# Query latents beside the first norm in a hybrid attention layer: the opening dealt anew

## The chip, the cores and the metric

The kernel runs on one core of one Trainium2 chip. The metric is the device time of one execution in microseconds; the time of a kernel is the median of its runs. Three runs of the kernel before took 2032.35, 2032.49 and 2034.26 us.

## What is computed

One layer of a streaming encoder on 1024 frames of width 1024, all in float32:

```
h  = rms_norm(x, ln_mix_pre)
z  = h @ w_in            # [q | k | v of 8 differential heads | q latent 384 | kv latent 256 | k rope 64 | 2 x 1024 gate logits]
branch A: 8 heads, o1 - lam * o2 of two softmax maps, rotary q and k, rms_norm per head
branch B: 8 heads from the latents: rms_norm(cq) @ w_uq, rms_norm(ckv) @ w_ukv, rotary part
x  = x + rms_norm((sigmoid(g_a) * (A @ w_proj_a) + sigmoid(g_b) * (B @ w_proj_b)) @ w_o)
x  = x + rms_norm((silu(h2 @ w_gate) * (h2 @ w_up)) @ w_down),   h2 = rms_norm(x)
```

Attention is causal by chunks of 64 frames. The change touches only the order in which the parts of z are made.

## The kernel before, in words

**Arithmetic.** Every float32 operand of a matmul is held as two fp32r parts: a high part, cast by ScalarE, and a low part, the rest, made by VectorE or POOL (`split_sbuf`, L252 to L256; `split_psum`, L258 to L261). One product is three matmuls, high by high, high by low, low by high (`mm3`, L266 to L269). So in the trace L267, L268 and L269 are the matmuls of nearly all projections, told apart by their columns: 384 for a differential head's projection and for the query latents, 320 for the kv latents, 512 for gate tiles.

**Memory.** Two large SBUF buffers, AR (split operands) and AFm (float32), are divided into zones. A zone hands out the piece that has been free for the longest time. Weights of projections come through `f_raw` (room for eight pieces of 384 columns) into `z_w` (8192 columns of AR); one set of eight 384-column weights takes 6144 of them. x tiles, tables, latents and other float32 pieces come from `f_gen`, 8448 columns. PSUM has eight banks: in the opening banks 0 to 5 serve the first head's projection, banks 6 and 7 all transposes. In the heads 0 to 3 hold scores, 4 and 5 projections.

**Order.** The parts are generators, written out by hand in the order wanted; the framework then fixes the order of every engine when the program is built, from the program's order, taking forward what it holds to be ready. Engines run their own lists in order, and all DMAs are issued from the one queue of SP, in order too.

**The opening.** `norm_x` goes through the eight x tiles of 128 rows, from 7 down to 0: load, sum of squares (ScalarE, L439), 1/rms (VectorE L245, POOL L247), multiply (VectorE, L441), eight transposes on TensorE (L447), split of two banks into hT (L260, L261). `rotary_tables` makes cosines and sines on VectorE in ten steps (L331 to L366). `da_proj(0)` projects the first differential head: eight weight pieces of 128 x 384, loaded at L546 as three strips of 128 columns and split with every second low half on POOL; then for each tile 24 matmuls, rotary steps on VectorE (`rope`, L385 to L390), splits, and transposes of K (L592). Before the change one step of the tables stands on either side of each tile of the norm, and then the projection is drained. `lambda_column` makes a scalar for the differential heads.

**The heads.** For each of the eight differential heads `interleave` runs the attention (first its small transposes at L689) together with fillers: gate tiles (48 matmuls of 512 columns each, with two weight pieces of 1024 columns), the query or the kv latents, and the projection of the next head. `FILL` names the fillers of each head, and a pace is summed from them: 10.4 for a gate tile, 33.6 and 28.0 for the latents, 32.4 for a projection. The pace only says how densely fillers stand between the attention's steps.

**The query latents.** `latents("cq")` loads eight weight pieces of 128 x 384 (L285), the latent norm's weights, and per tile does 24 matmuls, the sum of squares (L500), a multiply out of PSUM (L502), and, one tile later, three transposes (L518), a copy, and a store to the scratch s_cq in DRAM. The latents are read again only after the last differential head. All its low halves of weights are made by VectorE.

What follows the differential heads (the latent attention, the two branch projections, the output projection and the channel part) is not touched.

Of the kernel before, what the change touches and what calls it, by code (L numbers as in the profile page):

```python
# [21 lines left out]
NT = S // P  # L22
# [37 lines left out]

W_ENG = "dve"
L_ENG = lambda nc: nc.vector
FILL = ((0, 1, 2, 3), (4, 5), ("cq",), ("ckv",), (6, 7), (8, 9), (10, 11, 12), (13, 14, 15))
PRE = 1
DA_DEPTH = 1
MLA_DEPTH = 2
# [103 lines left out]
def kernel(  # L170
# [122 lines left out]
    mr, mf, mp = Mem(AR, AR_COLS), Mem(AFm, AF_COLS), Psum(PS)  # L293
# [18 lines left out]
    ps_s, ps_p, ps_a = Banks(mp, 0, 4), Banks(mp, 4, 6), Banks(mp, 6, 8)  # L312
# [166 lines left out]
        for o in own:  # L479
            o.free()  # L480

    def latents(which):
        if which == "cq":
            lo, n, nw, nrm, dst = 3072, 384, 384, q_a_norm, s_cq
        else:
# [3 lines left out]
        nc.sync.dma_start(wb.ap, nrm[0].partition_broadcast(P))  # L489
        nb = nw // P  # L490
        late = None
        for t in reversed(range(NT)):
            sl = slice(t * P, (t + 1) * P)
            pb = ps_p.alloc()
            o = pb.ap[:, 0:n]
            for k in range(NK):
                mm3(o, hT[:, k, 0, sl], hT[:, k, 1, sl], w[k][0], w[k][1], k == 0, k == NK - 1)
# [268 lines left out]
    def drain(g):  # L766
        for c in g:
            assert c != "blocked"
# [556 lines left out]
    all_slots = [[None] * 4 for _ in range(NH + 1)]  # L1325
    nx, tab = norm_x(), rotary_tables()
    next(nx)
    next(tab)
    next(nx)
    first = da_proj(0, all_slots[0], Banks(mp, 0, 6))  # L1330
    next(first)
    for _ in range(NT):
        next(tab, None)
        next(nx, None)
        next(tab, None)
    drain(tab)
    drain(nx)
    neg_lam, sub8 = lambda_column()
    drain(first)
    M = Mla()  # L1340
    hs = [{} for _ in range(NH + 1)]

# [4 lines left out]
    for n in range(NH):  # L1347
        fl, pace = [], 0.0
        for f in FILL[n]:
            if f == "cq":  # L1350
                fl.append(latents("cq"))
                pace += 33.6
            elif f == "ckv":
                fl.append(latents("ckv"))
                pace += 28.0
            else:
                fl.append(gate_tile(f))
                pace += 10.4
        if n == NH - 1:
            fl += [after_ht(), mla_setup(M), mla_proj(M, 0, hs[0])]  # L1360
            pace += 35.0
        if n + 1 < NH:
            fl.append(da_proj(n + 1, all_slots[n + 1]))
            pace += 32.4
        interleave(da_attn(n, all_slots[n], neg_lam, sub8), fl, pace)
# [72 lines left out]
```

## Time and profile before

| what | value |
|---|---|
| median of three runs | 2032.49 us |
| time of the profiled execution | 2036.9 us |
| its span, first to last instruction | 2035.0 us |
| mean granted TensorE clock | 0.992 |

Busy shares of the page, in order: TensorE's matmuls, its weight loads, VectorE, ScalarE, POOL. On TensorE a row of a matmul lasts until its result is out, so that rows of matmuls in a series overlap; the distance of two starts tells the pace. On the page and in the windows, PE is TensorE's matmuls, PEld its weight loads, DVE VectorE, ACT ScalarE, and POOL GpSimd. A number behind x is a count. Behind a windows row's stretch stand its length, then busy time and count of each engine, the granted clock as a share of 2.4 GHz (1.00 also where the trace has no record of it), the busy share of the DMA engines and GB/s.

### The profile page before, as it was taken

What the parts mean: (1) busy time and instruction counts of PE and PEld (TensorE: products, weight loads), DVE (VectorE), ACT (ScalarE), POOL (GpSimd) and SP (SyncE); (2) the same over time, 40 slices, a digit from 0 to 9 for tenths busy, and PEclk for the clock granted to TensorE, in tenths of its full rate; (3) what the DMA queues carried; (4) which work ended last, traced back from release to release, by engine and by line L of the source; (5) the groups of instructions that cost most, each with busy time, mean ns of one, the idle gap of its engine ahead of it and who ended that gap; (6) DMA issues with size and microseconds to landing.
All of it is one profiled execution on the core that took longest, in us unless ns stands there. A gap on an engine that the chain in (4) does not pass through costs nothing. (4 is left out here: it accounts for less than half of the span.)

```text
span 2035.0 us, 29108 instructions
## 1 busy us (share of the span) xinstructions
PE 1976.3 (97%) x10656; PEld 1715.3 (84%) x10656; DVE 1156.2 (57%) x2464; ACT 864.2 (42%) x1912; POOL 541.0 (27%) x652
## 2 busy tenths in 40 slices
PE   6999999999999999999999998979999999999998
PEld 6898999999898988988978786757888888888886
DVE  7756757676675667786752354575344444353335
ACT  5445444554544446666653333343333333341102
POOL 2000010200000012222121222356564564462214
PEclk9999999999999999999999999989999999999999
DMA  5212111211212031450043533223222222272204
GB/s 169 69 47 81 44 55 53 57 49 42 77 29 80 29 116 50 130 177 29 32 136 103 176 125 103 85 71 94 73 94 84 71 95 73 95 237 83 83 32 145
DMA packets 148494, 176.52 MB, mean 87 GB/s; under 512 B 13536, under 2 KB 117376, under 8 KB 148352
## 3 DMA queue, kind: packets, MB, share of 16 engines
q1 hardware_dynamic: 148352, 174.68, 27.3%
q8 instruction: 83, 1.36, 0.3%
q14 instruction: 59, 0.48, 0.1%
HBM read 130.54 MB, written 44.11 MB: 86 GB/s over the span
## 5 line engine op out<-in xcount | busy, mean ns | idle before, releaser
L267 PE MATMUL PS<-AR 128*128 128x512 f32 (+3 forms) x2216 | 795.1, 361 | 4.0 <-ACT AR L254 2.5
L269 PE MATMUL PS<-AR 128*128 128x512 f32 (+3 forms) x2216 | 786.3, 356 | 2.6 <-POOL AR L256 2.6
L268 PE MATMUL PS<-AR 128*128 128x512 f32 (+3 forms) x2216 | 784.5, 355 | 3.7 <-POOL AR L256 3.7
L254 ACT CAST AR<-AFm 128x512 fp32r<-128x512 f32 (+4 forms) x514 | 301.7, 610 | 514.1 <-PE PS L1216 207.4
L267 PEld LDWEIGHTS PS<-AR 128*128 128x128 f32 x2216 | 418.1, 189 | 56.8 <-ACT AR L260 3.5
L268 PEld LDWEIGHTS PS<-AR 128*128 128x128 f32 x2216 | 419.0, 189 | 47.8 <-POOL AR L256 4.5
L269 PEld LDWEIGHTS PS<-AR 128*128 128x128 f32 x2216 | 417.9, 189 | 46.3 <-POOL AR L256 3.5
L256 POOL TENSOR_TENSOR AR<-AFm,AR 128x512 fp32r<-128x512 f32 (+4 forms) x203 | 309.2, 1529 | 461.7 <-ACT AR L254 397.4
L1216 PE MATMUL PS<-AR 128*128 128x512 f32 x1848 | 425.7, 392 | 6.1 <-POOL AR L256 4.9
L1216 PEld LDWEIGHTS PS<-AR 128*128 128x128 f32 x1848 | 349.3, 189 | 82.2 <-POOL AR L256 6.2
L256 DVE TENSOR_TENSOR AR<-AFm,AR 128x512 fp32r<-128x512 f32 (+5 forms) x311 | 213.1, 714 | 109.3 <-ACT AR L254 81.8
L260 ACT CAST AR<-PS 128x512 fp32r<-128x512 f32 (+3 forms) x320 | 134.5, 440 | 149.5 <-DVE AFm L388 75.4
L1225 DVE TENSOR_TENSOR AFm<-AFm,PS 128x512 f32<-128x512 f32 x110 | 75.2, 684 | 180.3 <-PE PS L1216 179.6
L261 DVE TENSOR_TENSOR AR<-PS,AR 128x512 fp32r<-128x512 f32 (+3 forms) x320 | 152.9, 496 | 38.0 <-ACT AR L260 36.5
L619 POOL CAST AR<-AR 128x128 fp32r<-128x128 f32 (+1 forms) x128 | 43.1, 337 | 456.0 <-PE PS L690 262.4
L649 ACT ACTIVATE AFm<-PS,nm 128x1024 f32<-128x1024 f32 (+3 forms) x192 | 142.5, 745 | 45.9 <-DVE nm L648 28.8
L648 DVE TENSOR_REDUCE nm<-PS 128x1 f32<-128x1024 f32 (+3 forms) x192 | 143.5, 751 | 3.2
L1288 DVE TENSOR_TENSOR AFm<-AFm,PS 128x512 f32<-128x512 f32 x80 | 54.4, 685 | 103.1 <-PE PS L269 103.1
L1180 DVE TENSOR_TENSOR AFm<-AFm 128x512 f32<-128x512 f32 x66 | 70.4, 1066 | 68.4 <-DMA s_aa<-AFm 29.7
L627 POOL MEMSET AR<- 128x256 f32 x64 | 22.3, 349 | 295.3 <-PE PS L269 200.3
L707 PE MATMUL PS<-AR 128*128 128x256 f32 x640 | 94.9, 290 | 0.1
L609 PE MATMUL PS<-idf,AFm 128*128 128x128 f32 x576 | 88.6, 275 | 2.2 <-ACT AFm L741 0.9
(133 smaller groups left out, 1551.9 us busy)
## 6 DMA issues: line engine op xcount, KB each, us to landing
AFm<-in_w_in_dram SPq DMA_DIRECT2D x72, 192.0 KB
AFm<-in_w_ffn_gate_dram SPq DMA_DIRECT2D x22, 512.0 KB
AFm<-in_w_ffn_up_dram SPq DMA_DIRECT2D x22, 512.0 KB
s_aa<-AFm SPq DMA_DIRECT2D x44, 256.0 KB
AFm<-in_w_ffn_down_dram SPq DMA_DIRECT2D x22, 512.0 KB
AFm<-s_aa SPq DMA_DIRECT2D x22, 512.0 KB
AFm<-in_x_dram SPq DMA_DIRECT2D x16, 512.0 KB
AFm<-in_w_in_dram SPq DMA_DIRECT2D x32, 256.0 KB
```

Source lines behind the costliest of these rows:

```text
L254: nc.scalar.copy(h, src)
L256: e.tensor_tensor(out=l, in0=src, in1=f32v(h), op=ALU.subtract)
L260: nc.scalar.copy(h, src)
L261: nc.vector.tensor_tensor(out=l, in0=src, in1=f32v(h), op=ALU.subtract)
L267: nc.tensor.matmul(o, lhsT=sh, rhs=mh, start=first, stop=False)
L268: nc.tensor.matmul(o, lhsT=sh, rhs=ml, start=False, stop=False)
L269: nc.tensor.matmul(o, lhsT=sl, rhs=mh, start=False, stop=last)
L609: nc.tensor.transpose(tb.ap[:, q * P:(q + 1) * P], C[:, (g + q) * P:(g + q + 1) * P], idf)
L648: nc.vector.tensor_reduce(out=nm[:, m:m + 1], in_=src, axis=ax, op=ALU.max, negate=True)
L649: nc.scalar.activation(out=dst, in_=src, func=ACTF.Exp, bias=nm[:, m:m + 1], scale=1.0, accum_out=ss[:, m:m + 1])
L707: nc.tensor.matmul(sb.ap[:, p * 256:(p + 1) * 256], lhsT=qs.ap[:, m * 256 + v * P:m * 256 + v * P + P], rhs=slots[p]["kT"][:, m, :], start ...
L1216: nc.tensor.matmul(o, lhsT=v[:, ws, k], rhs=m, start=first and k == 0 and x == 0, stop=k == 3 and x == 2, skip_group_check=True)
```

## The change

The query latents leave the fillers of the third head and go into the opening. They are loaded ahead of the norm's first tile, take six PSUM banks, and one tile of latents stands behind each tile of the norm. The tables start behind the second tile and take two steps behind each tile from the third on. The first differential head's projection, its weights' loads included, comes after all that. The gate tiles are dealt anew.

```diff
-FILL = ((0, 1, 2, 3), (4, 5), ("cq",), ("ckv",), (6, 7), (8, 9), (10, 11, 12), (13, 14, 15))
+FILL = ((0, 1, 2), (3, 4), (5, 6), ("ckv",), (7, 8), (9, 10), (11, 12), (13, 14, 15))
...
-    def latents(which):
+    def latents(which, banks=None):
+        banks = banks or ps_p
...
         nc.sync.dma_start(wb.ap, nrm[0].partition_broadcast(P))
         nb = nw // P
         late = None
+        if which == "cq":
+            yield 0.0
         for t in reversed(range(NT)):
             sl = slice(t * P, (t + 1) * P)
-            pb = ps_p.alloc()
+            pb = banks.alloc()
...
     nx, tab = norm_x(), rotary_tables()
     next(nx)
-    next(tab)
+    first = latents("cq", Banks(mp, 0, 6))
+    next(first)
     next(nx)
-    first = da_proj(0, all_slots[0], Banks(mp, 0, 6))
-    next(first)
-    for _ in range(NT):
-        next(tab, None)
+    for t in range(NT):
         next(nx, None)
-        next(tab, None)
+        next(first, None)
+        if t == 1:
+            next(tab)
+        elif t > 1:
+            next(tab, None)
+            next(tab, None)
+    drain(nx)
     drain(tab)
-    drain(nx)
+    drain(first)
     neg_lam, sub8 = lambda_column()
-    drain(first)
+    drain(da_proj(0, all_slots[0], Banks(mp, 0, 6)))
```

## Rows read from the trace of the kernel before

**Rows 1.** The page, part 1: busy us, share of the span, instructions

```profile
PE 1976.3 (97%) x10656; PEld 1715.3 (84%) x10656; DVE 1156.2 (57%) x2464; ACT 864.2 (42%) x1912; POOL 541.0 (27%) x652
```

**Rows 2.** Windows of the opening: stretch, PE, PEld, DVE, ACT, POOL, clock, DMA

```profile
0.00:11.75 11.75, 0.00 (x0) 0.00 (x1) 5.00 (x17) 4.54 (x8) 1.61 (x10) 1.00 0.81 227
11.75:16.81 5.06, 2.80 (x10) 2.07 (x10) 4.61 (x7) 3.60 (x8) 4.97 (x4) 1.00 1.08 333
16.81:21.09 4.28, 4.28 (x16) 4.18 (x17) 3.66 (x6) 2.22 (x5) 1.16 (x2) 1.00 0.34 114
21.09:61.57 40.48, 38.83 (x239) 37.12 (x239) 36.08 (x102) 22.65 (x50) 6.50 (x14) 1.00 0.32 93
```

**Rows 3.** Timeline of TensorE, 0 to 21 us: start, us, engine, line, operation

```profile
11.75 1.97 PE L447 MATMUL PS<-idf,AFm 128*128 128x128 f32 x8 [11.75 <-DVE rs_v L245]
...
16.81 1.12 PE L447 MATMUL PS<-idf,AFm 128*128 128x128 f32 x4 [2.26 <-DVE AR L261]
...
20.50 0.52 PE L269 MATMUL PS<-AR 128*128 128x384 f32 x1
...
20.82 0.47 PE L267 MATMUL PS<-AR 128*128 128x384 f32 x1
```

**Rows 4.** Windows cut at the starts of heads 0, 1, 2, 4, 5, 6

```profile
61.57:170.31 108.74, 108.67 (x643) 97.59 (x642) 68.48 (x191) 48.48 (x129) 5.52 (x18) 1.00 0.22 66
170.31:252.80 82.49, 82.49 (x527) 76.53 (x527) 56.77 (x158) 41.20 (x110) 5.93 (x21) 1.00 0.19 58
252.80:351.40 98.60, 97.28 (x647) 93.83 (x647) 63.80 (x177) 48.85 (x136) 9.74 (x29) 1.00 0.19 52
...
446.10:529.10 83.00, 83.00 (x524) 76.17 (x523) 56.24 (x156) 41.58 (x109) 6.20 (x21) 1.00 0.18 53
529.10:611.30 82.20, 82.20 (x520) 75.64 (x519) 55.93 (x155) 40.74 (x107) 5.77 (x20) 1.00 0.18 53
611.30:705.20 93.90, 93.65 (x569) 84.76 (x569) 56.79 (x156) 42.55 (x110) 5.75 (x21) 1.00 0.19 56
```

**Rows 5.** Timeline of TensorE, 24 to 62 us, for the pitch

```profile
24.10 1.04 PE L447 MATMUL PS<-idf,AFm 128*128 128x128 f32 x8
...
24.89 0.42 PE L267 MATMUL PS<-AR 128*128 128x384 f32 x1
...
60.35 0.34 PE L269 MATMUL PS<-AR 128*128 128x384 f32 x1
...
61.57 0.39 PE L267 MATMUL PS<-AR 128*128 128x512 f32 x1
```

**Rows 6.** First loads: the timeline of SP and ScalarE, and one window

```profile
2.27 0.43 SPq L432 DMA_DIRECT2D AFm<-in_ln_mix_pre_dram  x1
4.51 1.06 ACT L439 ACTIVATE AFm<-AFm 128x1024 f32<-128x1024 f32 x1 [2.50 <-DMA AFm<-in_x_dram]
7.50:12.00 4.50, 0.25 (x1) 0.25 (x2) 4.36 (x15) 2.36 (x5) 0.75 (x2) 1.00 1.14 325
```

**Rows 7.** Lines by form on VectorE, 0 to 46 us: busy us, mean ns

```profile
L441 DVE SCALAR_TENSOR_TENSOR AFm<-AFm,rs_r 128x1024 f32<-128x1024 f32 x7 | 9.7, 1386 | 1.9 <-POOL rs_r L247 1.8
L261 DVE TENSOR_TENSOR AR<-PS,AR 128x512 fp32r<-128x512 f32 x14 | 9.3, 683 | 0.7 <-ACT AR L260 0.6
L350 DVE SCALAR_TENSOR_TENSOR AFm<-AFm 128x256 f32<-128x256 f32 x15 | 6.2, 415 | 0.0
L256 DVE TENSOR_TENSOR AR<-AFm,AR 128x384 fp32r<-128x384 f32 x4 | 3.5, 888 | 0.0
L345 DVE SCALAR_TENSOR_TENSOR AFm<-AFm 128x256 f32<-128x256 f32 x6 | 2.5, 419 | 0.1
...
L366 DVE TENSOR_SCALAR AFm<-AFm 128x256 f32<-128x256 f32 x4 | 1.1, 286 | 0.6 <-ACT AFm L355 0.6
...
L359 DVE TENSOR_SCALAR AFm<-AFm 128x256 f32<-128x256 f32 x1 | 0.3, 284 | 0.0
```

**Rows 8.** L502, the latents' multiply: duration ns, and its waits (both latents)

```profile
L502 DVE SCALAR_TENSOR_TENSOR AFm<-PS,rs_r,AFm x8: 618/618/620, 255.7 to 301.8; 128x384 f32<-128x384 f32 x8
...
  POOL rs_r L247: 8.7, 14
```

**Rows 9.** One window of the latent attention's end, columns as in rows 2

```profile
1030.00:1040.00 10.00, 7.86 (x36) 6.31 (x36) 3.35 (x8) 4.27 (x10) 3.94 (x7) 0.74 0.66 198
```

**Rows 10.** Timeline of POOL in the opening: low halves of weights

```profile
12.81 5.16 POOL L256 TENSOR_TENSOR AR<-AFm,AR 128x384 fp32r<-128x384 f32 x4
```

## The prediction

> **What bounds the kernel now.** I read the page first, then the windows of the opening, its timeline, and last the windows cut at the starts of the eight differential heads. The page shows TensorE busy 97% of the span, VectorE 57% [rows 1], so only TensorE's lost time can be won, and the reader is to look for where it is lost. The windows show it in one place: before 11.75 us it does nothing, from 11.75 to 16.81 it is busy for 2.80 us, and then it hardly stops: 38.83 of 40.48 us up to 61.57, where the first gate tile begins [rows 2]. The heads behind it show TensorE busy in all but 1.3 us of the worst of them [rows 4]. A busy matmul row overlaps the next, so I count pitches, start to start: seven of 128x384 take from 60.35 to 61.57, 0.174 us each, and eight transposes of an x tile 24.10 to 24.89, 0.10 us each [rows 5].
>
> The opening's timeline shows why its first 21 us are poor: transposes at 11.75, a wait of 2.26 us for VectorE's low halves before 16.81, and matmuls at 0.32 us (20.50 to 20.82) where later ones take 0.174 [rows 3]. This is TensorE at 1.2 GHz in place of 2.4: the windows print 1.00 there because no clock record precedes 21.09, and the pitch is the evidence. By 21.09, 26 instructions are done [rows 2], 16 of them transposes: 16 x 0.10 + 10 x 0.174 = 3.3 us of work, so 17.8 us are lost. The whole opening holds 192 matmuls and 64 transposes, 33.4 + 6.4 = 39.8 us; 61.57 - 39.8 = **21.8 us lost before**, 4.0 of them behind 21.09 (the small transposes of K are in this, the same in both kernels).
>
> **The change, part by part.** The total of matmuls stays the same. The 192 matmuls and 24 transposes of the query latents, 33.4 + 2.4 = 35.8 us, go from head 2 to the opening; the first head's projection stands behind them; gates are 3,2,2,0,2,2,2,3 over the heads instead of 4,2,0,0,2,2,3,3.
>
> Out of the heads. Three heads with two gate tiles and a projection take 82.49, 83.00 and 82.20 us, mean 82.56; one with three takes 93.90 [rows 4]: a gate tile costs 11.34, a head without any 59.9. Head 2, latents and no gate, takes 98.60, so the latents cost 38.7 there, 2.9 more than their work. The sixteen gate tiles are only moved, each at 11.34: head 0 loses one, head 6 one, head 2 gains two, sum zero. Head 0 with its start takes 108.74 against 82.56 + 22.7 = 105.2; I leave its 3.5 us as they are, since no row shows a head 0 with three, and bound what it may do by 1.5 either way (less than half of it). The pace numbers that go with them only spread fillers in heads whose TensorE has no idle time to fill.
>
> Into the opening, its start. SP now issues x tile 7, eight weight loads of 192 KB, the q norm's row (192 KB) and only then the norm's weights (512 KB) and x tile 6; before, the norm's weights went out at 2.27 us, ahead of the projection's. Tile 7 was there at 4.51 [rows 6]. Behind it 1.5 + 0.19 + 0.5 = 2.2 MB at the 325 GB/s of 7.5 to 12 us [rows 6] take 6.8 us, so the norm's weights land at about 11.2; the multiply of 1.39 us [rows 7], its end overlapped a little, leads to transposes at 12.4, where 11.75 was. Against this, the weights' splits are done by then (all eight low halves on VectorE, twice the 3.5 us of the four of before [rows 7], while it would wait for the norm's weights; POOL's four took 5.16 us from 12.81 on [rows 10], past the first tile's transposes), the positions' two loads and the tables' first operations stand later, and the 2.26 us wait should go: VectorE's two low halves follow the casts directly.
> Transposes 12.4 to 14.4, then slow matmuls until the clock rises. It rose 4.3 us after TensorE became dense (16.81 to 21.09), 9.3 us after its first instruction. With the first, 16.7: lost 12.4 + 1.2 (slow transposes) + half of 2.3 = 14.7. With the second, and transposes at 13.5 (290 GB/s; the windows show 227, the empty first 2 us in it, to 333 [rows 2]): 18.4. I take 16.5, the middle, as no row says which of the two counts. Of TensorE's ten instructions before 16.81, eight were transposes. The Trainium skill (TensorE: Matmul & The Clock Gate, Part 4: PE-mode transpose) states that transposes do not count as busy for the clock gate in the way matmuls do; by that rule the 4.3 us would run from 14.4, and the loss would be 1.0 us above that of the early rise, 15.7, inside the two ends. The rows of 11.75 to 21.09 agree with it as far as eight transposes at 11.75 brought no rise within 4.3 us, but their wait explains that as well.
>
> Into the opening, the steady part. Per x tile TensorE now has 24 x 0.174 + 11 x 0.10 = 5.3 us. VectorE has the multiply (1.39), two low halves (1.37), the latents' multiply out of PSUM (0.62), a wait for POOL's power before each of the two multiplies (8.7 us in 14 times, 0.6 each): 4.6 us; the tables add 6.2 + 2.5 us and ten smaller groups of 5.8 together (the first and the last stand in the rows), 14.5 over six tiles or 2.4 a tile [rows 7, 8]. That is 7.0 against 5.3 if nothing overlaps; but the tables run inside those waits, and before the change VectorE was busy 36.08 of 40.48 us [rows 2] with rotary work besides, while TensorE lost 4.0. So stalls of 2 (half of those) to 8 (0.8 on each tile and the seam's 1.6) us; I take 4.5: the 4.0 of before, near which VectorE's load stands, and a little for the longer stretch.
> ScalarE and POOL: a square and a copy of 128x384 and one more power per tile, under 2 us of ScalarE's, hidden by 5.3. SP: eight stores of s_cq stand between x loads; a store waits for its copy, and x tiles queue behind it, but a tile's buffer comes free two tiles before it is needed, so 10 us cover them. PSUM: six banks take the latents, the pair behind them serves x and latents' transposes in turn; the latents' are wanted one tile later, 4.2 us of cover.
> The seam: projection weights 0 and 1 go to untouched space, 2 to 7 into that of latent weights 0 to 5, free when the last tile has read them, 4.2 to 1.2 us before its end. TensorE then wants one every 0.52 us. Splits keep up unless POOL's four (1.29 us each, [rows 10]) come last: nothing to 3 us, taken as nothing and covered in the 8 above. The projection itself runs with VectorE free of tables, so its rotary backlog behind 61.57 shrinks; TensorE was dense there, so that is worth nothing.
>
> **Sum.** Gate 0 starts at lost + 39.8 + 35.8, lost = 16.5 + 4.5 = 21.0: 96.6 against 61.57, 35.0 later. The heads give 38.7. Net 3.7 us less. The profiled execution took 2036.9 us (span 2035.0), 4.4 above the median of the runs; the difference is taken over to the median: 2032.5 - 3.7 = **2028.8**. Bounds: lost from 14.7 + 2 to 18.4 + 8 is 8.0 less to 1.7 more; head 0 adds 1.5 either way. Behind 1000 us there are stretches at a granted clock of half (1030 to 1040 shows 0.74 [rows 9]) where TensorE was starved; a shift of the work may lengthen or shorten one, 2 us either way.
>
> **The rivals.** A measurement of this kernel tells about 0.2%, 4.1 us, from no change.
> *The opening becomes dense at once*: early rise, 14.7, and stalls of 2.5. Lost 17.2, 7.5 us less, 2025.0. For it: the wait of 2.26 us and the tables' VectorE work ahead of the first tile go. Against: the norm's weights come later.
> *VectorE paces the opening*: the tables do not fit into the waits, and its work stands end to end: eight tiles of 4.6, the tables' 14.5 and four low halves of the projection's weights, 3.5 [rows 7], are 54.8 us where TensorE's eight tiles need 42.4. Stalls of 12.4 in place of 4.5: lost 28.9, 4.2 more, 2036.7; with the late rise 2038.6. It decides from 42.4 us of VectorE in these tiles. For it: 7.0 against 5.3 in six of them. Against: VectorE's rows overlap by nearly 0.1 us each, waits and tables fill each other, and a heavier load cost 4.0 before.
> *Nothing comes of it*: the latents find as many stalls beside the norm as in head 2 (2.9) on top of the 4.0, and the late rise: lost 18.4 + 6.9 = 25.3, 0.6 more, 2033.1.
>
> **Chances.** My forecast, a gain under 4.1 us with the values taken: 0.42. Dense at once, beyond 4.1 us: 0.39. Nothing: 0.10, within 0.2%. VectorE paces: 0.09, slower. So faster 0.39, same 0.52, slower 0.09. The likeliest single result stays inside 0.2%, on the faster side. Its own range is 2028.4 to 2032; the range for 8 in 10 goes from 2022.5 (8.0 and 1.5 less) to 2036.0 (the dear opening of 1.7, and the shifts above).
>
> **What would show it.** Right: gate 0's first 128x512 matmul near 96.6 us; first x transposes near 12.4 with no gap of 2 us behind; head 2 near 82.6; head 0 near 97.4 from gate 0; tables finished on VectorE before the last x tile. Wrong: transposes that wait for VectorE's multiply on tiles 5 to 0; a hole of some us where the projection's first matmuls wait for POOL's or ScalarE's splits; a first tile delayed past 13.5 by its weights; heads of two gates that take other than 82 to 83 us. The forecast fails altogether if a head with moved gates costs more than 11.3 us a tile.

## The result, and the profile after

The changed kernel takes 2045.88 us (median of 4 runs, 2041.59 to 2048.61); beside it the kernel before took 2033.38 (2032.35 to 2034.68). The ratio is 1.0060, 95% interval 1.0048 to 1.0072: 12.5 us slower, where 3.7 less had been forecast. The profiled execution took 2046.58 us, its span 2044.4, 9.4 more than the span before. Medians and ratios here and below leave out one slow run, of e4, which took 7249.82 us.

The page, part 1, of the changed kernel, and the windows of its opening cut where the stretches of [rows 2] have their counterparts:

```profile
PE 1977.3 (97%) x10656; PEld 1713.5 (84%) x10656; DVE 1155.1 (56%) x2464; ACT 867.4 (42%) x1914; POOL 536.2 (26%) x652
```
```profile
0.00:12.50 12.50, 0.00 (x0) 0.00 (x0) 4.92 (x12) 6.33 (x11) 1.58 (x10) 1.00 0.86 289
12.50:15.00 2.50, 1.61 (x8) 1.57 (x8) 0.99 (x2) 1.61 (x3) 0.34 (x1) 1.00 1.05 330
15.00:21.40 6.40, 5.40 (x20) 4.62 (x19) 4.82 (x10) 2.71 (x6) 0.29 (x2) 1.00 0.49 108
21.40:60.00 38.60, 34.46 (x211) 32.00 (x210) 30.57 (x79) 20.45 (x45) 7.68 (x13) 1.00 0.38 109
60.00:104.22 44.22, 41.98 (x253) 41.02 (x252) 25.96 (x70) 15.40 (x43) 7.86 (x14) 1.00 0.21 57
```

The work is the same, engine by engine, as in [rows 1]; only where TensorE stands has changed. Gate 0 starts at 104.22 where 96.6 was forecast. The heads' windows, heads 0, 1, 2, 4, 5 and 6, answer to [rows 4]:

```profile
104.22:202.35 98.13, 97.92 (x593) 88.48 (x591) 62.07 (x172) 44.83 (x118) 5.20 (x19) 1.00 0.22 62
202.35:284.87 82.52, 82.52 (x522) 75.73 (x520) 56.18 (x156) 41.39 (x109) 6.13 (x22) 1.00 0.19 57
284.87:367.12 82.25, 82.25 (x530) 76.25 (x528) 56.16 (x158) 41.86 (x113) 5.64 (x20) 1.00 0.18 52
...
461.12:544.02 82.90, 82.68 (x521) 75.62 (x520) 56.17 (x156) 41.34 (x109) 5.96 (x20) 1.00 0.17 50
544.02:625.81 81.79, 81.79 (x519) 75.15 (x518) 56.51 (x156) 41.24 (x109) 5.85 (x21) 1.00 0.19 54
625.81:708.78 82.97, 82.96 (x524) 76.18 (x523) 55.20 (x153) 39.91 (x106) 6.00 (x21) 1.00 0.20 59
```

Head 0 takes 98.13 (97.4 forecast), head 2 82.25 (82.6), head 6 82.97 for 93.90 after its lost gate. The eight heads together go from 733.3 us (61.57 to 794.91) to 694.6 (104.22 to 798.80): 38.8 given back, 38.7 forecast. So the latent attention starts 42.7 - 38.8 = 3.9 us late. The other 5.5 us of the span come behind it, in stages that the change does not touch. Windows of the latent attention's first six heads, the stages from there to the last gate/up product, and the down projection with what follows, first of the kernel before, then of the changed one:

```profile
794.91:1001.70 206.79, 206.12 (x1366) 184.67 (x1365) 147.27 (x333) 133.35 (x322) 46.81 (x138) 1.00 0.27 89
1001.70:1786.04 784.34, 755.49 (x3416) 622.07 (x3415) 369.05 (x533) 286.94 (x504) 327.15 (x247) 0.98 0.31 99
1786.04:2025.78 239.74, 239.74 (x1058) 198.20 (x1056) 99.67 (x127) 53.71 (x82) 76.95 (x42) 1.00 0.34 112
```
```profile
798.80:1009.88 211.08, 207.03 (x1365) 184.65 (x1365) 147.63 (x333) 133.66 (x322) 45.56 (x138) 1.00 0.26 88
1009.88:1791.83 781.95, 754.65 (x3416) 621.37 (x3415) 368.33 (x532) 288.52 (x505) 327.59 (x248) 0.98 0.31 98
1791.83:2035.19 243.36, 240.05 (x1058) 198.12 (x1056) 96.08 (x127) 54.39 (x82) 75.00 (x41) 1.00 0.34 112
```

They add 4.3, take 2.4 back, and add 3.6. The 2.4 is no saving: the kernel before takes 784.34 us there in this profile and 779.14 in its second one (e6 below). The matmul counts stay within one; in the first window PE's busy time grows by 0.9 us and its idle time by 3.4, in the last 3.3 of the 3.6 are idle.

**Where the opening's time goes.** The waits of TensorE up to gate 0 (us in total, times, longest), and four rows of its timeline:

```profile
PE PS L447 <- DVE AFm L441: 18.1, 7, 13.4
PE PS L521 <- DVE AFm L505: 1.7, 1, 1.7
PE PS L447 <- DVE AR L261: 1.0, 1, 1.0
```
```profile
27.05 0.34 PE L267 MATMUL PS<-AR 128*128 128x384 f32 x1
28.30 1.09 PE L447 MATMUL PS<-idf,AFm 128*128 128x128 f32 x8 [0.92 <-DVE AFm L441]
29.16 0.42 PE L268 MATMUL PS<-AR 128*128 128x384 f32 x1
...
29.95 0.34 PE L269 MATMUL PS<-AR 128*128 128x384 f32 x1
```

The first of the seven waits for the norm's multiply is the start, 13.39 us (12.4 forecast). Six more stand before later x tiles, 0.6 to 0.9 us each, 4.7 in sum: TensorE stands at a later tile's transposes, with the latents of the present tile not yet done. Of their 24 matmuls 19 lie ahead of the transposes shown and five behind them (29.16 to 29.95); in the next four waits it is six, four, five and five. These few run behind the transposes without a wait and take 0.17 us each, so their 0.7 to 1.0 us would about have filled waits of 0.65 to 0.92, had they stood ahead in TensorE's list. No run tried that. What the six waits are for is read on ScalarE and VectorE just ahead of one of them:

```profile
24.12 0.49 ACT L503 ACTIVATE AFm<-PS 128x384 f32<-128x384 f32 x1 [2.88 <-PE PS L269]
...
24.61 1.05 ACT L439 ACTIVATE AFm<-AFm 128x1024 f32<-128x1024 f32 x1
```
```profile
25.62 0.62 DVE L505 SCALAR_TENSOR_TENSOR AFm<-PS,rs_r,AFm 128x384 f32<-128x384 f32 x1 [0.66 <-POOL rs_r L247]
26.15 0.14 DVE L245 TENSOR_SCALAR rs_v<-ss 128x1 f32<-128x1 f32 x1
26.96 1.28 DVE L441 SCALAR_TENSOR_TENSOR AFm<-AFm,rs_r 128x1024 f32<-128x1024 f32 x1 [0.67 <-POOL rs_r L247]
```

ScalarE sits 2.88 us in front of the latents' square L503, which needs the end of a group of matmuls, and the norm's square L439 of a later x tile stands right behind it in ScalarE's list. From 24.12 the chain runs L503, L439, L245, POOL's power, L441, to 28.24: 4.1 us, in which TensorE's matmuls ahead of the transposes last only to 27.39. On VectorE the norm's L245 also stands behind the latents' L505, which waits for POOL; that is 0.4 us of the chain. The norm is thereby tied to the latents that it should run ahead of.

### The profile page after: what moved, and what is told of

It reads as the page before. It is cut to its first block, busy times and chain, and to the rows that moved or that the text cites. A ratio compares the mean times of both kernels' runs of the same rounds, so it can differ in the third digit from the quotient of the medians.

```text
span 2044.4 us, 29103 instructions
## 1 busy us (share of the span) xinstructions
PE 1977.3 (97%) x10656; PEld 1713.5 (84%) x10656; DVE 1155.1 (56%) x2464; ACT 867.4 (42%) x1914; POOL 536.2 (26%) x652
## 5 line engine op out<-in xcount | busy, mean ns | idle before, releaser
L267 PE MATMUL PS<-AR 128*128 128x512 f32 (+3 forms) x2216 | 795.7, 362 | 14.7 <-ACT AR L254 10.4
L254 ACT CAST AR<-AFm 128x512 fp32r<-128x512 f32 (+6 forms) x514 | 301.7, 610 | 517.6 <-PE PS L1219 205.3
L267 PEld LDWEIGHTS PS<-AR 128*128 128x128 f32 x2216 | 418.8, 189 | 69.1 <-ACT AR L254 11.8
L260 ACT CAST AR<-PS 128x512 fp32r<-128x512 f32 (+2 forms) x320 | 134.4, 440 | 162.9 <-DVE AFm L388 85.4
L261 DVE TENSOR_TENSOR AR<-PS,AR 128x512 fp32r<-128x512 f32 (+2 forms) x320 | 152.7, 497 | 38.9 <-ACT AR L260 37.5
L652 ACT ACTIVATE AFm<-PS,nm 128x1024 f32<-128x1024 f32 (+3 forms) x192 | 142.6, 745 | 46.8 <-DVE nm L651 32.3
L1183 DVE TENSOR_TENSOR AFm<-AFm 128x512 f32<-128x512 f32 x66 | 68.2, 1033 | 66.0 <-DMA s_aa<-AFm 28.9
L612 PE MATMUL PS<-idf,AFm 128*128 128x128 f32 x576 | 88.9, 275 | 1.9 <-DVE AFm L942 1.0
```

The source lines that it names most:

```text
L254: nc.scalar.copy(h, src)
L260: nc.scalar.copy(h, src)
L261: nc.vector.tensor_tensor(out=l, in0=src, in1=f32v(h), op=ALU.subtract)
L267: nc.tensor.matmul(o, lhsT=sh, rhs=mh, start=first, stop=False)
L612: nc.tensor.transpose(tb.ap[:, q * P:(q + 1) * P], C[:, (g + q) * P:(g + q + 1) * P], idf)
L652: nc.scalar.activation(out=dst, in_=src, func=ACTF.Exp, bias=nm[:, m:m + 1], scale=1.0, accum_out=ss[:, m:m + 1])
```

## The experiments

The diffs are against the changed kernel unless another is named; "gate 0" is the start of the first 128x512 matmul.

**e1: the norm one more tile ahead; e2: the tables behind the norm; e3: the latents behind the norm; e4: the old deal of gates.** Each is one edit.

```diff
# e1: in the opening, a third step of the norm
     next(nx)
+    next(nx)
     for t in range(NT):
# e2: the tables are only drained, behind the norm
-        if t == 1:
-            next(tab)
-        elif t > 1:
-            next(tab, None)
-            next(tab, None)
# e3: no tile of latents is placed in the loop; they are drained behind it
         next(nx, None)
-        next(first, None)
# e4
-FILL = ((0, 1, 2), (3, 4), (5, 6), ("ckv",), (7, 8), (9, 10), (11, 12), (13, 14, 15))
+FILL = ((0, 1, 2, 3), (4, 5), (), ("ckv",), (6, 7), (8, 9), (10, 11, 12), (13, 14, 15))
```

> The norm runs one x tile further ahead of the latents; every engine has the same work. Theory A (lock step: in ScalarE's list the next tile's sum of squares stands behind the sum of squares of the latents of the tile that TensorE is just finishing, so the whole chain to the next transposes starts too late by about 1 us a tile): TensorE's waits for the multiply L441 behind the first tile fall from 4.7 us to under 1.5, the first gate tile's matmul comes at 98 to 100.5 us instead of 104.2, the median 3.5 to 6 us below that of the changed kernel. Theory B (VectorE's work in the tiles, tables included, paces the opening): gate tile still at 103 to 105, same time.

Measured: 2044.91 us, ratio 1.0055 (1.0040 to 1.0070). Gate 0 at 104.33, and the waits for L441 behind the first one are still 17.9 - 13.2 = 4.7 us. Theory A's figures are missed and those of theory B are met. But the edit did not undo the lock step that A names: in e1's trace the norm's square still stands right behind the latents' (L439 at 25.95 behind L503 at 25.47, 32.81 behind 32.34). So e1 shows that one more x tile in hand does not help, and decides nothing between A and B.

> The tables' steps are taken out of the norm's tiles and stand behind the whole norm; ScalarE's list keeps the order of the two sums of squares. Theory A (lock step): the waits for L441 stay at 4 to 5.5 us in six tiles, first gate tile at 102.5 to 105 us. Theory B (VectorE paces): some 14 us of VectorE work leave the tiles, the waits fall under 1.5 us and the first gate tile comes at 97 to 100 us.

Measured: 2047.92 us, ratio 1.0069 (1.0054 to 1.0084), gate 0 at 107.73. With no tables among the tiles the waits are the same to 0.2 us (TensorE's waits up to gate 0):

```profile
PE PS L447 <- DVE AFm L441: 18.1, 7, 13.6
PE PS L521 <- DVE AFm L505: 3.0, 1, 3.0
```

So VectorE's tables do not make these waits, and theory B, which gave 97 to 100 us, falls. Gate 0 came 3.5 us later than in the changed kernel, outside theory A's range too; 1.3 of it stand before L521.

> The latents stand behind the whole norm in the program's order, so that the norm goes first on every engine and TensorE fills with latents, as it filled with the first head's projection before the change. Theory A (lock step): waits for L441 behind the first tile under 1.5 us, first gate tile at 97 to 100 us, median 4 to 7 us below that of the changed kernel. Theory B: 103 to 105 us, same time.

Measured: gate 0 at 101.96, later than theory A's 97 to 100, and the six waits are gone (13.9 us in two waits, 13.8 of it the start):

```profile
PE PS L447 <- DVE AFm L441: 13.9, 2, 13.8
```

Only 2.3 us of it reach gate 0: waits for low halves (L261, 2.2) and for the last latents (L521, 2.5) grow. The whole is dearer all the same, 2050.18 us, ratio 1.0089 (1.0070 to 1.0107): head 7 takes 94.4 us for the changed kernel's 90.0, and TensorE waits 9.6 us at the start of the down projection. Two windows of that stretch in e3:

```profile
1797.00:1807.00 10.00, 1.75 (x8) 1.13 (x6) 3.70 (x3) 4.19 (x4) 4.60 (x2) 0.85 0.79 278
1807.00:1817.00 10.00, 8.61 (x25) 6.41 (x26) 2.45 (x2) 8.32 (x12) 7.10 (x4) 0.63 0.79 269
```

TensorE is nearly idle in the first, and in the second it is granted a mean of 0.63: behind the wait, matmuls of 512 columns go out every 0.43 us (1809 to 1814) in place of 0.23. The stage takes 252.7 us, 12.9 more than in the kernel before: 9.6 of wait, and 3.3 behind it.

> The opening is that of the changed kernel; the gate tiles are dealt as before the change, with no filler but the projection in the third head. Theory C (a gate tile costs 11.3 us in any head, the dealing is worth nothing): third head at 59 to 61 us, start of the latent attention within 1 us of the 798.8 of the changed kernel, same time within 0.2%. Rival D (the dealing matters: a head without fillers starves TensorE, or a head with four is dearer): start of the latent attention off by 2 us or more.

Measured: 2040.18 us, ratio 1.0031 (1.0020 to 1.0042). The latent attention starts at 799.61, as in the changed kernel (798.80): ahead of it the deal is worth nothing, as forecast. But the whole is 5 to 6 us cheaper, and the latent attention's window is as in the kernel before:

```profile
799.61:1006.79 207.18, 206.50 (x1365) 184.70 (x1365) 147.31 (x333) 133.62 (x322) 47.26 (x138) 1.00 0.27 88
```

When the order of TensorE's instructions in the traces is compared from the latent attention on, by source line and shape, e4's is that of the kernel before, instruction by instruction; the changed kernel's differs in 43 places (e9's expectation counts 45 in the built lists), 28 of them in the latent attention's first six heads, although no line of those stages was edited.

**e5 and e6: the changed kernel and the kernel before, once more.**

> The changed kernel once more, one profile. Theory L (behind the opening the time goes to waits at places that the program's fixed order makes): TensorE idles again by 1.3 to 2.3 us each in the second and the fourth head of the latent attention, where the first profile had 1.7 and 1.8, and by 1 us or more behind the start of the down projection, where it had 3.3. Rival N (chance of one execution): these waits stand elsewhere or are gone.

> The kernel before once more, one profile. Theory L: under 0.3 us of idle TensorE in the second and fourth head of the latent attention and none behind the start of the down projection, as in the first profile; first gate tile again within 0.5 us of 61.6. Rival N: waits of 1 us or more appear there too.

Measured: e5 2042.26 us, e6 2031.95. In both profiles of the changed kernel the same instructions of the latent attention wait: in the profile after and in e5 the L267 at 917 waits 1.5 us for the softmax's L652, and the transposes L612 at 841 wait 1.0 and 0.5. In neither profile of the kernel before does TensorE wait in those places, and neither has an idle TensorE at the start of the down projection, where the changed kernel has 3.3 and 1.7 us. These waits belong to the program, not to one execution. Their sizes vary by up to 1.6 us.

The time of the stages between is less fixed. Window of e6 to set beside the 784.34 us of the kernel before, and its ten us of [rows 9]:

```profile
1001.94:1781.08 779.14, 752.23 (x3416) 620.09 (x3414) 371.02 (x533) 287.12 (x504) 327.84 (x247) 0.99 0.31 99
1030.00:1040.00 10.00, 8.36 (x48) 6.74 (x49) 5.16 (x12) 6.41 (x14) 4.80 (x7) 1.00 0.69 207
```

TensorE runs the same list in both, 5.2 us apart. From 1030 to 1040 us the first profile was granted 0.74 and this one 1.00; between 1020 and 1050 us it gains 3.1 of the 5.2. From e6 to e5 the six heads take 3.2 us more, the stages between 0.7, the down projection 2.0.

**e7: the deal alone, on the kernel before, whose opening it keeps.**

```diff
# against the kernel before
-FILL = ((0, 1, 2, 3), (4, 5), ("cq",), ("ckv",), (6, 7), (8, 9), (10, 11, 12), (13, 14, 15))
+FILL = ((0, 1, 2), (3, 4), ("cq", 5), ("ckv",), (6, 7), (8, 9), (10, 11, 12), (13, 14, 15))
```

> The kernel before with its opening, with the query latents left in the third head and one gate tile each moved out of the first and the sixth dealing (3, 2, latents and 1, kv latents, 2, 2, 3, 3). Every operation is the same. Theory C with L (a moved tile costs 11.3 us in any head; what else changes is the order that is fixed behind it): first gate tile at 61.6, start of the latent attention within 1.5 us of the 794.9 of before, and any difference of the whole beyond that, up to 6 us either way, is idle TensorE in the latent attention or at the start of the down projection. Rival O (only the opening can cost): the whole within 0.1% of the kernel before.

Measured: 2050.54 us, ratio 1.0073 (1.0054 to 1.0092), although gate 0 stands at 62.05. Both expectations are missed: the latent attention starts 7.2 us late, at 802.06, and the whole is 16.9 us dearer, where 1.5 and 6 were the bounds. Head 0 takes 98.9 and head 2 108.6 us, near 97.4 and 98.6 + 11.3. The cost comes later: head 7, whose fillers were not touched, takes 96.4 us for 89.7, with 4.8 idle; the latent attention's six heads 211.4 for 206.8; the down projection 244.8 for 239.8. A gate tile moved between two early heads costs more than the whole opening's failure, through stages it has nothing to do with.

**e8: the opening mended in three places.** The norm's weights and the second x tile are issued ahead of the latents' weights; the latents stand behind the norm in the program; their last transposes come when the projection of head 0 has been started.

```diff
# in latents, behind the loop over tiles
-        late()
-        wb.free()
         for o in own:
             o.free()
+        if which == "cq":
+            yield 0.0
+        late()
+        wb.free()
...
     next(nx)
+    next(nx)
     first = latents("cq", Banks(mp, 0, 6))
     next(first)
-    next(nx)
     for t in range(NT):
         next(nx, None)
-        next(first, None)
...
-    drain(first)
     neg_lam, sub8 = lambda_column()
-    drain(da_proj(0, all_slots[0], Banks(mp, 0, 6)))
+    for t in range(NT + 1):
+        next(first)
+    head = da_proj(0, all_slots[0], Banks(mp, 0, 6))
+    for _ in range(3):
+        next(head)
+    drain(first)
+    drain(head)
```

> The changed kernel with the norm's weights and the second x tile loaded ahead of the latents' weights, the latents behind the norm in the program's order, and the transposes of the last latents tile behind the first tile of the first head's projection. Theory A (order of TensorE's list and the late norm weights are what the opening loses): first x transposes at 11.5 to 12.3 us, no wait of over 1 us before the transposes of latents, first gate tile at 97 to 99.5 us, start of the latent attention 2 to 5 us before that of the changed kernel if no wait appears on the way. Rival B2 (VectorE and ScalarE are full and hold the opening at its length): first gate tile at 101 us or later.

Measured: gate 0 at 94.72, 9.5 us earlier than in the changed kernel and ahead of the expected 97 to 99.5; rival B2, which gave 101 or later, falls. TensorE's windows, and its waits up to gate 0:

```profile
0.00:12.50 12.50, 1.98 (x9) 1.58 (x9) 4.47 (x10) 7.08 (x13) 1.58 (x10) 1.00 0.87 266
...
21.40:60.00 38.60, 36.95 (x229) 34.81 (x228) 34.03 (x85) 23.48 (x56) 10.86 (x16) 1.00 0.41 123
60.00:94.72 34.72, 34.72 (x209) 34.43 (x208) 19.35 (x62) 9.36 (x31) 4.03 (x10) 1.00 0.19 52
```
```profile
PE PS L447 <- DVE AFm L441: 8.7, 3, 7.9
PE PS L267 <- ACT AR L260: 2.7, 1, 2.7
```

The first transposes stand at 7.85 instead of 13.39, the later waits for L441 shrink from 4.7 to 0.8, and the wait before L521 from 1.7 to 0.3. The latent attention starts at 791.04, 3.9 us before the kernel before. And the whole is still no better: 2036.48 us over 10 runs, ratio 1.0014 (1.0005 to 1.0024). The latent attention's six heads take 210.7, the down projection 242.8: the late losses, 3.9 and 3.1 us, stayed.

**e10 and e12: two of e8's three mends by themselves.** e10 is the first (`next(nx)` moved ahead of the latents), e12 the last.

> The changed kernel with one thing moved: the norm's weights and the second x tile are loaded ahead of the latents' eight weight pieces. Theory A: first x transposes at 9 to 12 us in place of 13.4, the first gate tile 1.5 to 4 us earlier than 104.2 to 104.7; the waits for the multiply in the later tiles stay at 3.5 to 5.5 us. Rival: the clock's rise or the weights' arrival takes it all back, first gate tile within 0.7 us of the changed kernel.

> The changed kernel with one thing moved: the transposes of the last latents tile stand behind the first tile of the first head's projection. Theory A: the wait of 1.7 us before them goes under 0.5, the first gate tile 1.2 to 2 us earlier than 104.2 to 104.7. Rival: TensorE waits for the projection's weights there anyway, first gate tile within 0.7 us of the changed kernel.

Measured, one run each: gate 0 at 102.38 and 102.28, 1.8 and 1.9 us earlier. In e10 the first wait falls to 7.9 and the later ones stay, 12.5 - 7.9 = 4.6. In e12 the wait before L521 is gone and those for L441 stay. With e3's 2.3 that is 6.0 us one by one, 9.5 together. Part of it is that a mend alone leaves TensorE to meet other waits: e10's start is 5.5 us earlier, and 2.5 us of wait for a cast (L260) and 0.8 more before L521 come in. Part is scatter: five profiles with the changed kernel's opening (its own, e4, e5, e14, e18) have gate 0 between 104.02 and 104.81. The wholes were 2052.86 and 2039.58 us, 13 us apart at the same gate 0; their down projections take 253.1 and 239.8.

**e9 and e11: e8 with other deals**, chosen because TensorE's order lies nearer to that of the kernel before (6 differences from the latent attention on in e9) or the loads at the end come in another order (e11).

```diff
# against e8
-FILL = ((0, 1, 2), (3, 4), (5, 6), ("ckv",), (7, 8), (9, 10), (11, 12), (13, 14, 15))
+FILL = ((0, 1, 2), (3, 4), (5,), ('ckv',), (6, 7), (8, 9), (10, 11, 12), (13, 14, 15))       # e9
+FILL = ((0, 1), (2, 3), ('ckv',), (4, 5), (6, 7), (8, 9), (10, 11, 12), (13, 14, 15))        # e11
```

> The opening of the norm-first kernel with gate tiles dealt 3, 2, 1, kv latents, 2, 2, 3, 3, chosen because TensorE's list from the latent attention on is then all but that of the kernel before (six places differ; 43 in the norm-first kernel, 45 in the changed one); the loads at the start of the down projection still stand in another order. Theory L (what is lost behind the heads hangs on the order that is fixed there): first gate tile at 94 to 95.5 us, start of the latent attention at 790 to 793, idle TensorE in the latent attention's eight heads under 3 us in all as in the kernel before (2.6), the start of the down projection idle by 0 to 4; the median 0 to 4 us below the kernel before. Rival P (the new opening itself disturbs what follows, through the state of buffers and DMA): idle time in the latent attention's second to fourth head of 2 us or more as in the norm-first kernel, median above the kernel before.

> The opening of the norm-first kernel with the gate tiles dealt 2, 2, kv latents, 2, 2, 2, 3, 3. Theory L: the same first gate tile (94 to 95.5 us) and start of the latent attention (within 2 us of 791.0), and a whole that differs from the norm-first kernel's by idle TensorE at other places behind it, 5 us or less either way. Rival C2 (only the deal's place in the heads counts): the difference to the norm-first kernel is made before the latent attention starts.

Measured: e9 2040.45 us, ratio 1.0037 (1.0025 to 1.0049). Its latent attention is that of the kernel before, head by head to 0.1 us:

```profile
791.89:998.71 206.82, 206.15 (x1365) 184.66 (x1365) 147.23 (x333) 133.50 (x322) 47.27 (x138) 1.00 0.27 89
```

Over all kernels, these six heads take 206.8 to 207.2 us where TensorE's list for them is that of the kernel before (that kernel itself, e4, e9, and e15 below), and 206.3 to 211.4 where it is another: 210.0 to 211.4 in eight kernels with 28, 29 or 57 differences in these heads (the changed kernel, e3, e7, e8, e12, and e13, e14 and e18 below), 206.3 to 209.2 in e1, e2, e10, e11, e16 and e17, with 8 to 76. The same order gives the same time; another order can cost 4 us, or nothing, and the number of differences does not tell which. But e9's down projection starts with 9.5 us of idle TensorE, where 0 to 4 were expected, and the whole is 7.3 us above the kernel before where 0 to 4 below it was expected. e11 took 2033.88 us over 10 runs, ratio 1.0005 (0.9996 to 1.0014): gate 0 at 94.70, latent attention from 790.49, and 4.7 us idle at the down projection.

**e13 to e16: low halves of the down projection's activations on VectorE**, in e8, in the changed kernel, in the kernel before and in e11. In e9 SP's loads there wait 16.7 us for POOL's low halves, which hold the raw slots.

```diff
-            aa.append(load_hl(s_aa[f * P:(f + 1) * P, :], f_dn, z_dn, S))
+            aa.append(load_hl(s_aa[f * P:(f + 1) * P, :], f_dn, z_dn, S, eng="dve"))
```

> The norm-first kernel, with one more edit: the low halves of the down projection's activations are made by VectorE instead of POOL. Theory S (TensorE stands at the start of that stage because loads wait for raw slots that POOL's low halves hold, each 1 to 2 us longer than VectorE's): no stall there, the stage from the last gate/up product to TensorE's end takes 239.8 to 240.5 us instead of 242.8, everything ahead of it as in the norm-first kernel (gate 0 at 94.7, latent attention from 791.0), and the whole about 3 us less than it: about 2033.5 us, the kernel before's time within 2 us. Theory R (the order of instructions and DMAs of that stage is drawn anew by any edit, POOL or not): the stage takes anything from 239.8 to 253 us, and the four kernels of this call differ in it by over 3 us.

> The changed kernel with the low halves of the down projection's activations on VectorE. Theory S: the stage takes 239.8 to 240.5 us instead of 241.8 to 243.4, the whole about 2042 to 2043.5 us, with the losses ahead (gate 0 at 104.2, latent attention 208 to 212 us) unchanged. Theory R: the stage takes anything from 239.8 to 253 us.

> The kernel before with the low halves of the down projection's activations on VectorE. Theory S: no stall to take away, the stage stays at 239.8 us and the whole at 2033.4 within 1 us. Theory R: the order of that stage is drawn anew here too, and it takes up to 13 us more than 239.8.

> The norm-first kernel with the other deal of gate tiles, and the low halves of the down projection's activations on VectorE. Theory S: the stage takes 239.8 to 240.5 us instead of 247.6 and the whole about 2026 us, 7 us under the kernel before. Theory R: the stage takes anything from 239.8 to 253 us, the whole 2026 to 2039.

Measured: e13 2036.73 us, ratio 1.0015 (1.0005 to 1.0024); e14 2044.39, 1.0046 (1.0033 to 1.0060); e15 2033.53, 0.9999 (0.9990 to 1.0008); e16 2030.54 over 11 runs, 0.9981 (0.9972 to 0.9990). TensorE's wait at the start of the stage is 3.3, 1.0, 0 and 1.8 us, the stage 245.0, 241.2, 239.8 and 243.6. In e13 and e16 it is the row

```profile
PE PS L267 <- ACT AR L254: 3.3, 1, 3.3
```
```profile
PE PS L267 <- ACT AR L254: 1.8, 1, 1.8
```

Theory S foresaw no wait anywhere. It falls as the whole cause: less wait in two of three, not less in e13, and e14's 1.0 is not far from the 1.7 of e5, which is the changed kernel itself. The control loses nothing, against theory R's draw by any edit. e16 is the one kernel of the study that beats both, by 3.4 us (0.19% by the ratio), with an interval that leaves 1 out. It is the best of many orders tried, and nothing here says which would be good before it is run.

**e17 and e18: stores of the gate/up results from POOL's queue**, in e16 and in the changed kernel. In SP's one list the loads of the stage stand behind stores that wait for POOL's multiply, 32.7 us of such waits in the changed kernel (1745 to 1800).

```diff
-                        nc.sync.dma_start(s_aa[r:r + P, c * 512:(c + 1) * 512], s.ap)
+                        nc.gpsimd.dma_start(s_aa[r:r + P, c * 512:(c + 1) * 512], s.ap)
```

> The other-deal kernel with VectorE's low halves (e16), and one more edit: the stores of the gate/up results to s_aa are issued from POOL's queue, not SP's. Theory Q (the stall at the start of the down projection is SP's one queue: its loads of w_down and s_aa stand behind stores that wait for POOL's multiply, 5.5 us in e16 and 32.7 us in the changed kernel over those stretches): no idle TensorE there, the stage takes 239.8 to 240.5 us instead of 243.6, and the whole 3 to 4 us less than e16, about 2027 us. Rival T (the loads land late because the DMA engines and the round trip through s_aa set it, whatever the queue): the stage keeps 1 to 5 us of idle TensorE and the whole stays within 2 us of 2030.5, or gets slower by what POOL's issuing adds.

> The changed kernel with one edit: the stores of the gate/up results to s_aa are issued from POOL's queue, not SP's. Nothing ahead of the gate/up stage should move by over 1 us. Theory Q: the stage from the last gate/up product to TensorE's end falls from 241.8 to 243.4 us to 239.8 to 240.5, and the whole to about 2042 to 2043. Rival T: the stage keeps 1 to 5 us of idle TensorE.

Measured: 2053.65 us, ratio 1.0111 (1.0093 to 1.0129), and 2068.21, 1.0177 (1.0160 to 1.0194). The idle time at the start of the down projection stays, 2.8 and 3.7 us: theory Q falls, rival T's expectation holds. The loss, not foreseen in its size, is in the gate/up stage, 459.0 and 457.0 us for 433.1 and 434.3. In e17, 9.2 of the 25.9 us are PE's busy time (433.4 for 424.2), the rest idle time, most of it waits for VectorE (1345 to 1775, where e16 has one of 0.9):

```profile
PE PS L1221 <- DVE AFm L1230: 16.1, 10, 1.9
```

## Why the prediction was wrong

**Heads: right.** 38.8 given back for 38.7; head 0 at 98.13 within its bound; a gate tile moved costs what it costs anywhere, up to the last head (e4). Nothing was lost at the seam's splits; what held it was another wait, L521 for the last latents' multiply, 1.7 us with the first projection matmuls queued behind it in TensorE's list. The cost of a gate tile says nothing of what its moving does further down: in e7 head 7 took 6.7 us more, with the same fillers.

**The opening's start: the size, inside its ends.** By 21.40 the changed kernel has done 16 transposes and 12 matmuls, 3.7 us of work: 17.7 lost, 16.5 taken, 14.7 to 18.4 the ends. Transposes at 13.39, near the later price. The multiply starts at 12.05, when the norm's weights have landed, 0.85 later than the 11.2 of the sum. The 2.26 us wait for low halves, which was to go, left 1.0 (L261). That the size fell between its ends is in part luck: when the clock rises is not fixed by the program (below).

**The opening's steady part: the step that failed.** Behind 21.40 there are 82.8 us for 75.6 - 3.7 = 71.9 us of work: 10.9 lost, where 4.5 was taken with 2 to 8 as ends. Waits are 6.4 of it, the six of 4.7 and the 1.7 before L521; the other 4.5, in which TensorE counts as busy, are about what was taken. The forecast's own sign of being wrong, transposes that wait for VectorE's multiply on later tiles, came true. The sentence "a tile's buffer comes free two tiles before it is needed" was the wrong test: x tiles were there (e1), and the sum of VectorE's work, set against TensorE's, did not matter (e2; VectorE is busy 30.57 of 38.60 us in the window shown). ScalarE's part had been costed at "under 2 us of ScalarE's, hidden by 5.3", as load; its place was not looked at. The square of the latents waits for matmuls, and the norm's next square queues behind it, so a chain of 4.1 us runs while TensorE has 3.3 us of matmuls ahead of the next transposes. Taking the latents out from among the norm's tiles removes just these waits (e3: 4.7 to 0.1, e8: to 0.8), which shows it as far as the place in the program goes; neither ScalarE's order nor TensorE's was changed by itself, so their shares are argued from the trace. The rival "VectorE paces" gave 28.9 us lost and 28.6 were measured, but by another mechanism: the number is no support for it.

**Behind the heads: the assumption that failed.** "2 us either way" was allowed for, by stretches of half clock getting longer or shorter; the spans show 5.5 more, e5 against e6 5.9. The cause had no sentence: the lists of all engines are fixed when the program is built, by what the framework holds to be ready, so an edit in the opening or in the deal of an early head rearranges lists a thousand microseconds later. With TensorE's order kept, the latent attention's six heads cost 207 in four kernels of four; with the changed kernel's 28 differences 210 to 211. This is shown as a connection between order and time, no more. Which of the moved places makes each wait was not taken apart, and of the 4.3 us 0.9 are PE's busy time, not idle.

**The sum by the trace.** 7.6 late at gate 0 on the forecast's -3.7 is the 3.9 at the latent attention; 4.3 - 2.4 + 3.6 make 9.4 of span. The medians differ by 12.5. The first profile of the kernel before is itself 4.4 us above its median, and against its second one, e6, that excess stands in the stages between (784.34 for 779.14). The pair e5 and e6 stand 10.0 apart in span: 4.2 at the latent attention, 3.2 in its six heads, 0.7 and 2.0 behind them. The rest of the 12.5 lies within the 7 us over which the four runs of the changed kernel scatter. The forecast's range, by its own terms, goes from 2023.0 to 2036.2 and not from 2022.5 to 2036.0; the measured time lies beyond either.

**What stays open.** At the start of the down projection TensorE idles 0 us in the kernel before, in e15 and in e12, and 1 to 10 us in the others, waiting for casts whose operands have not landed; the order of the loads of w_down, the stores and the loads of s_aa differs among them, and is the same in both executions of one kernel. POOL's hold on raw slots is at most a part (e13). With SP's stores out of its way the wait stayed (e17, e18), though the gate/up stage ahead of it had changed too. Head 7, from 89.5 us to 96.4 in e7, varies likewise and was not taken apart. What decides the order in which the loads come, and so the size, was not found.

**The clock.** The forecast chose between a rise reckoned from the first instruction and one reckoned from dense work. The runs bear out neither. In the changed kernel transposes come at 13.39 and the pitch of 0.32 us, the level of 1.2 GHz, ends at about 21.4; in e5, the same program, at 13.46 and 22.7. e8 and e9 have the same opening: transposes at 7.85 and 7.91, a wait, and matmuls without a stop from 12.48 and 12.35. Yet the pitch falls to 0.17 at 16.25 in e8 and at 18.66 in e9, and gate 0 stands at 94.72 and 95.75. So 2.4 us in the rise, or 1.0 at gate 0, come of nothing that the two openings do differently, and the middle between the two readings was as good as either. The Trainium skill (TensorE: Matmul & The Clock Gate, Part 4: PE-mode transpose) states that transposes do not count as busy as matmuls do. No run here decides on that: e8's early transposes are followed by a wait, and the scatter at gate 0 is as large as the 1.0 us that the rule made in the forecast.

## What to carry to other kernels

Where work is moved next to a chain through several engines, ask what stands next to what in each engine's list, not only whether the loads fit: a cheap instruction that waits for TensorE in front of the chain's first step ties the chain to it, and a step that stands a few instructions too early in the waiting engine's list can turn a hidden chain into a wait (argued here, not run). Where a framework orders the lists, an edit's price includes whatever it rearranges downstream; here that was worth up to 17 us (e7), more than the forecast gain, so compare the order of instructions in untouched stages with those of the kernel before, and give the range that width. A local gain seen in the trace (e8's 9.5 us at gate 0) is proved only when the whole is timed.

## What was not expected of the hardware

With stores issued from POOL, additions on VectorE became slower. The forms on VectorE, 1345 to 1775 us, whose operands all lie in SBUF (busy us, mean ns), first in e16, then in e17:

```profile
L1185 DVE TENSOR_TENSOR AFm<-AFm 128x512 f32<-128x512 f32 x64 | 66.2, 1035 | 65.9 <-DMA s_aa<-AFm 30.4 <-DMA AFm<-in_w_ffn_up_dram 18.7 <-issue 8.9
L256 DVE TENSOR_TENSOR AR<-AFm,AR 128x512 fp32r<-128x512 f32 x47 | 38.2, 814 | 2.0 <-ACT AR L254 1.7
```
```profile
L1185 DVE TENSOR_TENSOR AFm<-AFm 128x512 f32<-128x512 f32 x63 | 78.5, 1246 | 63.2 <-DMA s_aa<-AFm 43.2 <-DMA AFm<-in_w_ffn_up_dram 9.0 <-issue 5.8
...
L256 DVE TENSOR_TENSOR AR<-AFm,AR 128x512 fp32r<-128x512 f32 x45 | 45.4, 1009 | 2.8 <-ACT AR L254 2.5
```

Both grow by about 200 ns, while L1230, which reads PSUM, stays at 685 and 684. The traces show when. Two of e17's rows on VectorE, one with POOL idle (1506.50 to 1509.37), one with POOL at work on an operation of its own:

```profile
1508.01 0.69 DVE L256 TENSOR_TENSOR AR<-AFm,AR 128x512 fp32r<-128x512 f32 x1
...
1516.16 1.84 DVE L256 TENSOR_TENSOR AR<-AFm,AR 128x512 fp32r<-128x512 f32 x1
```
```profile
1516.16 1.29 POOL L1245 TENSOR_TENSOR AFm<-AFm 128x512 f32<-128x512 f32 x1
```

Sorted by what POOL does when they begin, the two forms take 0.68 to 0.69 us with POOL idle, in e16 and e17 alike (67 and 65 of them). While POOL runs an operation of its own they take 1.3 us on average in e16 (42 of them) and 1.8 in e17 (35), and the eight in e17 that begin while POOL issues a store take 2.19 each. A store's issue takes POOL 580 ns, 42 times between 1345 and 1800 us. That TensorE's waits in e17 come from this is likely, and no run tested it by itself.
